# A decoder layer in fp32 on one core: both gates' projections as seven half-size products instead of eight

## The chip, the core and the metric

One core of one Trainium2 chip runs the kernel. The metric is the device time of one execution in microseconds (us), the median over the runs; lower is better. The engines are called as in the profile: PE (matrix products; PEld is its loading of stationary operands), DVE (VectorE), ACT (ScalarE), POOL (GpSimd) and SP (here only a queue that issues transfers). Transfers go through queues of SP, ACT and POOL to 16 DMA engines; POOL's queue can add to the target (an accumulating transfer).

## The reference

One layer, 512 tokens (S), 2048 channels, all in fp32:

```python
h   = RMSNorm_pre(x)
[q | k | v | z_att | u | g_glu | z_conv] = h @ w_in      # 2048 x 7168, seven parts of 1024 columns
# group A: stick-breaking attention, 8 heads x 128
y_att  = attention(q, k, v) * silu(z_att)
# group B: GLU(u, g_glu) -> causal depthwise conv (31 taps) -> LayerNorm -> silu -> pointwise
y_conv = conv_module(u, g_glu) * silu(z_conv)
out = x + RMSNorm_post(concat(y_att, y_conv) @ w_out)
```

The change concerns `h @ z_att` and `h @ z_conv`, the two gates.

## The kernel before, in words

**Products.** PE multiplies in a reduced fp32 form. So each operand is split into a high part and the rest (`split`: ACT writes `h_*`, DVE subtracts and writes `l_*`), and a product is three matmuls (`mm3`): high by high, high by low, low by high. h is kept so in `h_hi` and `h_lo`, channels on partitions, 512 tokens in the free dimension.

**Steps.** The work of PE is a list of steps, each with a load and two units. A step's load brings 1 MB of weights by SP's queue into one of two buffers (`raws`), and splits it into one of two buffers each of `his` and `los`; the load of step n+1 is written ahead of the units of step n. `pair(c0, ...)` makes 256 output channels: channels on the partitions of the result, weights stationary (128x128), h streaming 512 tokens. A pair is two steps (two halves of the 2048 input channels) of 48 matmuls 128x512. Each gate is four pairs (`za0` to `za3` by `gates_a`, `zc0` to `zc3` by `gates_c`), so the gates are 16 steps and 768 matmuls. `post_za` takes a finished result through Silu on ACT and multiplies the attention's `o_raw` on POOL; `post_zc` puts Silu of the result into `szc`, which the pointwise product takes later.

**Strassen's products elsewhere.** The values v and the output product were made by Strassen's seven products already: the matrices are cut into 2x2 blocks, and seven products of sums of blocks take the place of eight. Sums of weights are made in DRAM (`plan_sums`) by POOL's queue, a copy and then an accumulating transfer for each 1 MB; `sum_next` writes the next one of a list where it is called, not ahead of the latest matmul. v's sums of h (`make_v_form`) are made in SBUF (`xw`) by DVE.

**Order.** PE's order is the order of the code. That of DVE, ACT and POOL comes from a scheduler, by priorities: loads have a high one, work in the background list `bgq` a low one (`LATER`). In `bgq` are the 30 taps for each of eight channel tiles of the conv (DVE, `acc`, L401) and the LayerNorm. Four entries are taken per unit before `n_norm`, two behind it. Attention for each head (`heads_run`) goes forward by one tick per unit. The steps follow each other so: u and g, q and k, the 14 steps of v, more of g, u, q, k (`heads(t)`, `conv_in(t)`), the gates from `za0`, `za1`, `zc0`, `za2`, then from `n_norm` `zc1`, `zc2`, `zc3`, `za3` with the LayerNorm beside, four pointwise steps (`pw`), and 28 steps of output products (`a` and others, weights `r_w`, sums `ws`).

Names in rows: `r_x`, `h_x`, `l_x` are a weight block x as loaded and its two parts; `vs`, `ws` are sums of weights for v and for the output; `gn`, `xT`, `gT` belong to the start; `sz` is a gate after Silu.

Of the kernel before, what the change touches and what calls it, by code (L numbers as in the profile page):

```python
# [16 lines left out]
P = 128  # L17
# [27 lines left out]
SUMS_FROM = 18  # L45
# [3 lines left out]
def hybrid_layer(  # L49
# [46 lines left out]
    def split(hi, lo, src, scale=None):  # L96
# [4 lines left out]
        else:  # L101
# [3 lines left out]
            )  # L105

# [281 lines left out]
    def post_u(c):  # L388
        def post(i, ps):
# [29 lines left out]
    def mean_of(src, name):  # L419

        hi, lo = late(f"{name}_hi", F32R), late(f"{name}_lo", F32R)
        split(hi, lo, src)
        ps = op2.tile([P, S], F32, tag="o2", name=f"ln_{name}")
        nc.tensor.matmul(ps, mean_w, hi, start=True, stop=False)
        nc.tensor.matmul(ps, mean_w, lo, start=False, stop=True)
        return ps

    def layer_norm():

        mu = mean_of(ln_sums[0], "mu")  # L430
        yield
# [9 lines left out]
        var = mean_of(sqs[0], "var")  # L441
        v, y, t = late("ln_v"), late("ln_y"), late("ln_t")
# [49 lines left out]
    def plan_sums(name, order, pairs, block):  # L492

        made, todo = {}, deque()
        for q in order:
            base, more = SUMS[q]
            for accumulate in (False, True):
                for p in range(pairs):
                    for kg in range(2):
                        def go(q=q, base=base, more=more, accumulate=accumulate, p=p, kg=kg):  # L500
                            if accumulate:
                                return nc.gpsimd.dma_start(
                                    made[q, p, kg], block(*more, p, kg), accum_op=ALU.add
                                )
# [27 lines left out]
    V_ORDER = (1, 2, 5, 6, 3, 7, 4)  # L532
# [14 lines left out]
    def make_v_form(q):  # L547

        tt = nc.vector.tensor_tensor
        for mi in range(2):  # L550
            for jj in range(2):
# [21 lines left out]
                v_form[q, mi, jj] = hi, lo  # L573
                split(hi, lo, f)
# [30 lines left out]
    def v_load(q, kg):  # L605
        name = f"v{q}{kg}"
        ahead = min(2000, tc.cur_priority - floor[0])
        with tc.high_priority(offset=ahead):
# [4 lines left out]
            split(hi, lo, raw)  # L613
        form = {(1, 0): 5, (2, 1): 6, (6, 1): 3, (3, 0): 7}.get((q, kg))
# [127 lines left out]
    def post_za(h):  # L742
        def post(i, ps):
            sz = t2(f"sz{h + i}")
            nc.scalar.activation(sz, ps, AF.Silu)
            o = o_raw[h + i]
            nc.gpsimd.tensor_tensor(out=o, in0=o, in1=sz, op=ALU.mult)
        return post

    szc = {}  # L750

    def post_zc(c):
        def post(i, ps):
            szc[c + i] = t2(f"szc{c + i}")
            nc.scalar.activation(szc[c + i], ps, AF.Silu)
        return post


    def pointwise(t):
        def unit(i):  # L760
            def go(w):
# [4 lines left out]
                for k in range(CT):  # L766
                    mm3(ps, (hi[:, k, cs], lo[:, k, cs]), (s_hi[k], s_lo[k]), k == 0, k == CT - 1)
                yc = szc[c]
                nc.vector.scalar_tensor_tensor(
                    out=yc, in0=ps, scalar=vec[:, c, V_PB : V_PB + 1], in1=yc,  # L770
# [252 lines left out]
    def gates_a(t):  # L1023
        pair(C_ZA + t * 256, post_za(2 * t), f"za{t}")
# [270 lines left out]
```

## Time and profile before

| what | us |
|---|---|
| median of 3 runs | 870.19 (869.29 to 872.12) |
| the profiled execution | 871.51 |
| its span | 869.8, granted clock 0.997 |
| PE busy | 855.0 (98%), 3894 instructions |
| DVE busy | 631.0 (73%) |
| ACT busy | 395.3 (45%) |
| POOL busy | 124.5 (14%) |
| the gates' stage (481.50 to 664.70) | 183.20 long: PE busy 183.20, DVE 97.80, ACT 84.34, DMA engines 0.49 of it |

The profile is of one execution, so its own time stands beside the span of its instructions. Busy shares are means over stages; what a stage can give is read from its own row. A matmul's record overlaps the next one's, so what it costs in a row of many is the distance of the starts.

### The profile page before, as it was taken

The page shows a single profiled execution, that of the slowest core. Times are in us where ns is not written, and L with a number is a line of the kernel's source. Part 1 is how long each engine was busy: PE and PEld are TensorE (multiplying, and loading weights), DVE is VectorE, ACT ScalarE, POOL GpSimd, SP SyncE. Part 2 cuts the span into 40 slices and gives each one's busy share as a digit, 9 for nine tenths or more (in the row PEclk, how much of TensorE's full clock was granted, in tenths as well). Part 3 has the DMA queues.
Part 4 walks back from the last instruction along what each step waited for, and adds up shares of the span by engine and source line. Part 5 has one row for each costly group of instructions (what it writes and reads, how often), then busy time and mean ns, then how long its engine had stood idle before and what let it go on. Part 6 is the DMA issues. An engine that isn't in the chain of part 4 may idle for free.

```text
span 869.8 us, 9834 instructions
## 1 busy us (share of the span) xinstructions
PE 855.0 (98%) x3894; PEld 710.0 (82%) x3894; DVE 631.0 (73%) x773; ACT 395.3 (45%) x452; POOL 124.5 (14%) x154
## 2 busy tenths in 40 slices
PE   9999998999999999999999999999999999999995
PEld 7888787888888888888888888888888888888884
DVE  4798799986797979879696984245643776458775
ACT  5785124644443544243422545235722346455542
POOL 0221100001202132203111323031001000000031
PEclk9999999999999999999999999999999999999998
DMA  8899964568578455874488547862232346556783
GB/s 324 250 272 283 281 158 160 185 207 302 173 181 174 165 193 145 179 189 165 145 192 165 176 157 183 175 162 97 93 101 97 98 154 233 194 194 250 289 279 101
DMA packets 87046, 163.58 MB, mean 188 GB/s; under 512 B 3014, under 2 KB 52434, under 8 KB 83224
## 3 DMA queue, kind: packets, MB, share of 16 engines
q1 hardware_dynamic: 69824, 110.12, 37.3%
q0 software_dynamic: 16864, 52.43, 26.1%
q8 instruction: 30, 0.49, 0.2%
q10 hardware_dynamic: 312, 0.40, 0.1%
q14 instruction: 16, 0.13, 0.0%
HBM read 158.75 MB, written 54.53 MB: 245 GB/s over the span
## 4 chain that ended last, share of the span: by engine, by line
PE 80%; DVE 10%; DMA 6%; ACT 2%; issue 1%; POOL 0%; DVEq 0%; ACTq 0%; POOLq 0%
PE za L342 3%; PE zc L342 3%; PE za L344 3%; PE a L940 3%; PE zc L344 3%; PE za L343 3%; PE a L942 3%; PE zc L343 3%; PE a L941 3%; DVE acc L401 3%; DVE l_v L100 3%; DMA r_k<-in_w_in_dram 3%; PE k L342 3%; PE q L344 3%; PE q L342 3%; PE u L344 3%
## 5 line engine op out<-in xcount | busy, mean ns | idle before, releaser
L401 DVE SCALAR_TENSOR_TENSOR acc<-hg,vec,acc 128x512 f32<-128x512 f32 x240 | 182.2, 759 | 6.8
L100 DVE TENSOR_TENSOR l_w<-r_w,h_w 128x2048 fp32r<-128x2048 f32 x28 | 64.1, 2291 | 41.9 <-ACT h_w L99 41.9
L99 ACT ACTIVATE h_w<-r_w 128x2048 fp32r<-128x2048 f32 x28 | 53.5, 1915 | 42.1 <-DMA r_w<-ws 11.8
L344 PE MATMUL k<-h_hi,l_k 128*128 128x512 f32 x128 | 50.1, 391 | 1.1 <-DVE l_k L100 1.1
L342 PE MATMUL u<-h_hi,h_u 128*128 128x512 f32 x128 | 50.3, 393 | 0.0
L342 PE MATMUL q<-h_hi,h_q 128*128 128x512 f32 x128 | 50.1, 392 | 0.0
L342 PE MATMUL k<-h_hi,h_k 128*128 128x512 f32 x128 | 50.0, 391 | 0.0
L342 PE MATMUL za<-h_hi,h_za 128*128 128x512 f32 x128 | 50.0, 390 | 0.0
L342 PE MATMUL zc<-h_hi,h_zc 128*128 128x512 f32 x128 | 49.9, 390 | 0.0
L344 PE MATMUL u<-h_hi,l_u 128*128 128x512 f32 x128 | 49.9, 390 | 0.0
L344 PE MATMUL q<-h_hi,l_q 128*128 128x512 f32 x128 | 49.9, 390 | 0.0
L344 PE MATMUL za<-h_hi,l_za 128*128 128x512 f32 x128 | 49.8, 389 | 0.0
L344 PE MATMUL zc<-h_hi,l_zc 128*128 128x512 f32 x128 | 49.8, 389 | 0.0
L343 PE MATMUL u<-h_lo,h_u 128*128 128x512 f32 x128 | 49.8, 389 | 0.0
L343 PE MATMUL k<-h_lo,h_k 128*128 128x512 f32 x128 | 49.8, 389 | 0.0
L343 PE MATMUL za<-h_lo,h_za 128*128 128x512 f32 x128 | 49.8, 389 | 0.0
L343 PE MATMUL q<-h_lo,h_q 128*128 128x512 f32 x128 | 49.8, 389 | 0.0
L343 PE MATMUL zc<-h_lo,h_zc 128*128 128x512 f32 x128 | 49.8, 389 | 0.0
L940 PE MATMUL a<-h_w,f_hi 128*128 128x512 f32 x128 | 49.8, 389 | 0.0
L941 PE MATMUL a<-l_w,f_hi 128*128 128x512 f32 x128 | 49.8, 389 | 0.0
L942 PE MATMUL a<-h_w,f_lo 128*128 128x512 f32 x128 | 49.8, 389 | 0.0
L671 POOL TENSOR_SCALAR_AFFINE_SELECT t<-t 128x128 f32<-128x128 f32 x64 | 35.7, 635 | 81.1 <-DVE t L694 48.2
(339 smaller groups left out, 2136.7 us busy)
## 6 DMA issues: line engine op xcount, KB each, us to landing
ws<-in_w_out_dram POOLq DMA_DIRECT2D x24, 1024.0 KB, 9.3
r_w<-ws SPq DMA_DIRECT2D x16, 1024.0 KB
vs<-in_w_in_dram POOLq DMA_DIRECT2D x12, 1024.0 KB, 12.9
r_w<-in_w_out_dram SPq DMA_DIRECT2D x12, 1024.0 KB
r_u<-in_w_in_dram SPq DMA_DIRECT2D x8, 1024.0 KB
r_q<-in_w_in_dram SPq DMA_DIRECT2D x8, 1024.0 KB
r_k<-in_w_in_dram SPq DMA_DIRECT2D x8, 1024.0 KB
r_v<-vs SPq DMA_DIRECT2D x8, 1024.0 KB
```

The costliest lines, as they stand in the source:

```text
L99: nc.scalar.activation(hi, src, AF.Copy)
L100: nc.vector.tensor_tensor(out=lo, in0=src, in1=f32(hi), op=ALU.subtract)
L342: nc.tensor.matmul(ps, wh, ah, start=first, stop=False)
L343: nc.tensor.matmul(ps, wh, al, start=False, stop=False)
L344: latest[0] = nc.tensor.matmul(ps, wl, ah, start=False, stop=last).ins
L401: bgq.append(lambda j=j: nc.vector.scalar_tensor_tensor(out=acc, in0=hg[:, j : j + S], scalar=vec[:, ct, j : j + 1], in1=acc, op0=ALU.mult ...
L671: nc.gpsimd.affine_select(out=blk, in_=blk, compare_op=ALU.is_gt, fill=0.0, base=0, pattern=[[-1, P]], channel_multiplier=1,)
L940: nc.tensor.matmul(ps, fh[:, kk, ts], hi[:, k, :], start=st, stop=False, skip_group_check=True)
L941: nc.tensor.matmul(ps, fh[:, kk, ts], lo[:, k, :], start=False, stop=False, skip_group_check=True)
L942: nc.tensor.matmul(ps, fl[:, kk, ts], hi[:, k, :], start=False, stop=en, skip_group_check=True)
```

## The change

Both gates are made by Strassen's seven products, in step: products of the first gate ("a") and the second ("c") alternate in an order that lets both use one sum of h (`Z_ORDER`). Each is two steps of 24 matmuls: 28 steps, 672 matmuls 128x512. Now h is stationary (128 tokens) and 512 columns of weights stream, so tokens lie on the partitions of the result. `z_done` combines results (copies on ACT, sums on DVE), and `turn_z` transposes the four finished blocks of a gate on PE, 64 transposes in 16 groups, each followed by Silu and, for gate a, two multiplications on POOL.

The sums of h that the products need (forms 5, 6, 3, 7) are those of v. They are written to DRAM when v makes them (`kept_form`, 16 transfers of 256 KB by ACT's queue), loaded again in the gates by SP (`load_form`, 16 transfers) and split in place over `h_hi` and `h_lo` (`split_form`).

Sums of weights: forms 5 and 7 afresh (`begin`, then `take_up`), form 6 and then 4 "grown" in the place of form 5 or 6 by one accumulating transfer after that was loaded. For v this leaves 12 transfers instead of 16, for the output 28 instead of 32, and the gates add 24. Besides: a weight block is split in two halves (`split_halves`) in v and in the gates; the first tap of each conv tile goes from DVE to ACT; `conv_in(3)` stands after `heads(3)`, so that the last two tiles' taps fall into the gates; the LayerNorm begins at the 16th of the gates' steps, its matmuls some entries after their operands; pointwise takes its channels in the order 2, 3, 0, 1; v begins with form 5.

```diff
+    def split_halves(hi, lo, src):
+        half = src.shape[1] // 2
+        for a in (0, half):
+            split(hi[:, a : a + half], lo[:, a : a + half], src[:, a : a + half])
...
-            bgq.append(lambda: nc.vector.tensor_scalar(
-                out=acc, in0=hg[:, 0:S], scalar1=vec[:, ct, 0:1],
+            bgq.append(lambda: nc.scalar.activation(
+                acc, hg[:, 0:S], AF.Identity, bias=vec[:, ct, V_CB : V_CB + 1],
...
+        grown = {SUMS[q][0]: q for q in (6, 4) if q not in fresh}
+        def loaded_sum(q, p, kg, queue):
+            if q in grown:
+                made[grown[q], p, kg] = made[q, p, kg]
+                queue.append(partial(take_up, grown[q], p, kg))
...
-    V_ORDER = (1, 2, 5, 6, 3, 7, 4)
+    V_ORDER = (5, 1, 2, 6, 3, 7, 4)
...
+                nc.scalar.dma_start(
+                    kept_form[q][:, 4 * jj : 4 * jj + 4, mi * P : (mi + 1) * P], f
+                )
                 split(hi, lo, f)
...
+    Z_ORDER = [(1, "a"), (2, "a"), (5, "a"), (1, "c"), (5, "c"), (2, "c")]
+    Z_ORDER += [(q, which) for q in (6, 3, 7, 4) for which in "ac"]
+    Z_FORMS = {
+        (1, "a", 1): (5, 0, 1), (5, "c", 1): (6, 0, 0), (6, "a", 1): (3, 2, 0), (6, "c", 1): (7, 0, 1),
+    }
...
+    def load_form(q, j0, half):
+        for n in range(4):
+            raw = t2(f"r_form{q}{n}").rearrange("p (k t) -> p k t", k=2)
+            with tc.high_priority(offset=LATER):
+                nc.sync.dma_start(raw, kept_form[q][:, 2 * n : 2 * n + 2, :])
+            splits.append((z_units[0] + 4, partial(split, h_hi[j][:, ks, ts], h_lo[j][:, ks, ts], raw)))
...
+    def z_load(q, which, kg):
+            nc.sync.dma_start(
+                raw, z_w(which)(*PLAIN[q], 0, kg) if q in PLAIN else z_sum[which][q, 0, kg]
+            )
+            split_halves(hi, lo, raw)
+        z_loaded[which](q, 0, kg, zgrow)
+        if (q, which, kg) in Z_FORMS:
+            load_form(*Z_FORMS[q, which, kg])
...
+    def z_done(q, which, i):
+        if q in (1, 5, 4):
+            nc.scalar.copy(nat(q), ps)
+        elif q == 2:
+            tt(out=nat(1), in0=ps, in1=nat(1), op=ALU.add)
+        elif q == 6:
+            tt(out=nat(6), in0=nat(5), in1=ps, op=ALU.subtract)
...
+    def turn_z():
+        for c in range(2):
+            for i in range(2):
+                nc.tensor.transpose(
+                    ps[:, c * 256 + i * P : c * 256 + (i + 1) * P],
+                    z_nat[base, which, i][:, (2 * c2 + c) * P : (2 * c2 + c + 1) * P], ident,
+                )
+        nc.scalar.activation(sz, ps, AF.Silu)
...
+            for k in range(4):
+                ah, al = h_at(4 * (j0 + kg) + k, t0, t0 + P)
+                nc.tensor.matmul(ps, ah, hi[:, k, :], start=st, stop=False, skip_group_check=True)
+                nc.tensor.matmul(ps, ah, lo[:, k, :], start=False, stop=False, skip_group_check=True)
+                latest[0] = nc.tensor.matmul(ps, al, hi[:, k, :], start=False, stop=en, skip_group_check=True).ins
...
     heads(2)
+    heads(3)
     conv_in(3)
-    heads(3)
-    gates_a(0)
...
-    gates_a(3)
+    n_gates = len(steps)
+    gates()
+    n_norm = n_gates + 8
+    n_ln = n_gates + 15
     n_in = len(steps)
-    for t in range(4):
+    for t in (2, 3, 0, 1):
...
-        if n >= SUMS_FROM:
-            sum_next(sumq)
+        if SUMS_FROM <= n < n_gates or n >= n_in:
+            sum_next(zsumq or sumq)
+            if n % 3 == 0 or n >= n_in:
+                sum_next(zsumq or sumq)
...
             sum_next(v_sumq)
+            sum_next(grow)
+            sum_next(zgrow)
```

What this does to the order of the instructions at three places.

DVE in the gates, before: behind the last taps its work is almost only the splits of the weight blocks `l_za..` and `l_zc..` (the two digits are pair and half), one of the attention's (`al7`) and the LayerNorm's.

```order
L100 TENSOR_TENSOR l_zc01_4027<-r_zc01_4025,h_zc01_4026 128x2048
L100 TENSOR_TENSOR l_za20_4099<-r_za20_4097,h_za20_4098 128x2048
L100 TENSOR_TENSOR al7_4093<-aT7_4081,ah7_4092 128x1280
L100 TENSOR_TENSOR l_za21_4173<-r_za21_4171,h_za21_4172 128x2048
L100 TENSOR_TENSOR mu_lo_4330<-ln_sum_1703,mu_hi_4329 128x512
L100 TENSOR_TENSOR l_zc10_4230<-r_zc10_4228,h_zc10_4229 128x2048
L100 TENSOR_TENSOR l_zc11_4300<-r_zc11_4298,h_zc11_4299 128x2048
```

And now, in the first half of the gates (the digits of `l_zc50` are product and half; `acc6`, `acc7` are the conv's taps of the last two tiles, `r_form60` a piece of form 6, which is split over `h_hi0` and `h_lo0`):

```order
L100 TENSOR_TENSOR l_zc50_4113<-r_zc50_4111,h_zc50_4112 128x1024 x2
L406 SCALAR_TENSOR_TENSOR acc6_3679<-hg6_3676,vec_126,acc6_3679 128x512
L406 SCALAR_TENSOR_TENSOR acc7_3711<-hg7_3708,vec_126,acc7_3711 128x512
L406 SCALAR_TENSOR_TENSOR acc6_3679<-hg6_3676,vec_126,acc6_3679 128x512
L406 SCALAR_TENSOR_TENSOR acc7_3711<-hg7_3708,vec_126,acc7_3711 128x512
L406 SCALAR_TENSOR_TENSOR acc6_3679<-hg6_3676,vec_126,acc6_3679 128x512
L406 SCALAR_TENSOR_TENSOR acc7_3711<-hg7_3708,vec_126,acc7_3711 128x512 x3
L100 TENSOR_TENSOR l_zc51_4171<-r_zc51_4169,h_zc51_4170 128x1024 x2
L406 SCALAR_TENSOR_TENSOR acc7_3711<-hg7_3708,vec_126,acc7_3711 128x512 x2
L100 TENSOR_TENSOR h_lo0_120<-r_form60_4177,h_hi0_116 128x2x256
L406 SCALAR_TENSOR_TENSOR acc7_3711<-hg7_3708,vec_126,acc7_3711 128x512
L100 TENSOR_TENSOR h_lo0_120<-r_form61_4179,h_hi0_116 128x2x256
```

The splits stand as two halves for every 24 matmuls of PE, and between them are now taps and pieces of forms, which stood elsewhere or nowhere.

PE between the two units of the step `zc50`, now: the last of the first unit's matmuls, a group of transposes of gate a's first finished block, and the second unit.

```order
L898 MATMUL zc50_4185<-h_zc50_4112,h_hi0_116 128x512
L899 MATMUL zc50_4185<-l_zc50_4113,h_hi0_116 128x512
L900 MATMUL zc50_4185<-h_zc50_4112,h_lo0_120 128x512
L872 MATMUL zTa00_4199<-ident_91,zna10_3801 128x128
L872 MATMUL zTa00_4199<-ident_91,zna11_3868 128x128
L872 MATMUL zTa00_4199<-ident_91,zna10_3801 128x128
L872 MATMUL zTa00_4199<-ident_91,zna11_3868 128x128
L898 MATMUL zc51_4208<-h_zc50_4112,h_hi0_116 128x512
```

Before, a unit was 24 matmuls of a pair and the next unit followed at once; now it is 12, with such a group after 16 of the units.

POOL from the end of the gates on, before: the last multiplications by the gate (`o4`, `o5`, then `o6`, `o7`), the LayerNorm's sums and then only the end of the program (`xr`).

```order
L502 DMA ws710_3847<-in_w_out_dram 512x1x512
L502 DMA ws711_3962<-in_w_out_dram 512x1x512
L747 TENSOR_TENSOR o4_3248<-o4_3248,sz4_4258 128x512
L747 TENSOR_TENSOR o5_3520<-o5_3520,sz5_4285 128x512
L438 TENSOR_TENSOR ln_sq0_4336<-ln_sq0_4336,ln_sq2_4338 128x512
L438 TENSOR_TENSOR ln_sq0_4336<-ln_sq0_4336,ln_sq4_4340 128x512
L438 TENSOR_TENSOR ln_sq0_4336<-ln_sq0_4336,ln_sq6_4342 128x512
L747 TENSOR_TENSOR o6_3922<-o6_3922,sz6_4830 128x512
L747 TENSOR_TENSOR o7_4168<-o7_4168,sz7_4857 128x512
L1011 TENSOR_TENSOR xr0_6081<-r_0_1_5493,xr0_6081 128x512
```

And now, behind the last multiplications, in the pointwise and first output steps:

```order
L885 TENSOR_TENSOR o3_2929<-o3_2929,sza11_5082 128x256
L513 DMA ws610_3475<-in_w_out_dram 512x1x512
L513 DMA ws611_3477<-in_w_out_dram 512x1x512
L518 DMA ws700_5196<-in_w_out_dram 512x1x512
L518 DMA ws701_5198<-in_w_out_dram 512x1x512
L518 DMA ws710_5260<-in_w_out_dram 512x1x512
L518 DMA ws711_5262<-in_w_out_dram 512x1x512
L513 DMA ws700_5196<-in_w_out_dram 512x1x512
L513 DMA ws701_5198<-in_w_out_dram 512x1x512
L513 DMA ws710_5260<-in_w_out_dram 512x1x512
L513 DMA ws711_5262<-in_w_out_dram 512x1x512
L513 DMA ws600_3338<-in_w_out_dram 512x1x512
```

Ten transfers of 1 MB (copies at L518, accumulations at L513) that stood before the gates' end stand there now, and four more accumulations follow them.

More of the change, by code (lines that the diff above doesn't have):

```diff
@@ L422, in mean_of, with finish @@
         split(hi, lo, src)
[L423 to L426, printed above, removed]
+        def finish():
+            ps = op2.tile([P, S], F32, tag="o2", name=f"ln_{name}")
+            nc.tensor.matmul(ps, mean_w, hi, start=True, stop=False)
+            nc.tensor.matmul(ps, mean_w, lo, start=False, stop=True)
+            return ps
+        return finish
     def layer_norm():
         mu = mean_of(ln_sums[0], "mu")
+        for _ in range(4):
+            yield
+        mu = mu()
         yield
@@ L441, in layer_norm @@
         var = mean_of(sqs[0], "var")
+        for _ in range(5):
+            yield
+        var = var()
         v, y, t = late("ln_v"), late("ln_y"), late("ln_t")
@@ new lines, in hybrid_layer @@
+    for which in "ac":
+        z_sum[which], todo, z_loaded[which] = plan_sums(f"z{which}", (5, 7), 1, z_w(which))
+        zsumq.extend(todo)
+    def load_form(q, j0, half):
+        ts = slice(half * (S // 2), (half + 1) * (S // 2))
+        for n in range(4):
+            raw = t2(f"r_form{q}{n}").rearrange("p (k t) -> p k t", k=2)
+            with tc.high_priority(offset=LATER):
+                nc.sync.dma_start(raw, kept_form[q][:, 2 * n : 2 * n + 2, :])
+            j, ks = j0 + n // 2, slice(n % 2 * 2, n % 2 * 2 + 2)
+            splits.append((
+                z_units[0] + 4, partial(split, h_hi[j][:, ks, ts], h_lo[j][:, ks, ts], raw)
+            ))
@@ new lines, in turn_z @@
+    def turn_z():
+        if not turns or turns[0][0] > z_units[0]:
+            return
+        _, which, base, c2, pr, half = turns.popleft()
+        ps = op2.tile([P, S], F32, tag="o2", name=f"zT{which}{pr}{half}")
+        for c in range(2):
[3 more added lines that the diff above has]
+                    z_nat[base, which, i][:, (2 * c2 + c) * P : (2 * c2 + c + 1) * P], ident,
+                )
+        sz = t2(f"sz{which}{pr}{half}")
+        nc.scalar.activation(sz, ps, AF.Silu)
+        sz = sz.rearrange("p (c t) -> p c t", c=2)
+        if which == "c":
+            szc[pr, half] = sz
+            return
+        ts = slice(half * 256, (half + 1) * 256)
+        for c in range(2):
+            o = o_raw[2 * pr + c][:, ts]
+            nc.gpsimd.tensor_tensor(out=o, in0=o, in1=sz[:, c, :], op=ALU.mult)
@@ L759, in pointwise, with gates @@
+    def gates():
+        for q, which in Z_ORDER:
+            for kg in range(2):
+                steps.append(Step(
+                    lambda q=q, which=which, kg=kg: z_load(q, which, kg),
+                    [z_unit(q, which, kg, 0), z_unit(q, which, kg, 1)],
+                ))
     def pointwise(t):
@@ L767, in go @@
                     mm3(ps, (hi[:, k, cs], lo[:, k, cs]), (s_hi[k], s_lo[k]), k == 0, k == CT - 1)
-                yc = szc[c]
-                nc.vector.scalar_tensor_tensor(
-                    out=yc, in0=ps, scalar=vec[:, c, V_PB : V_PB + 1], in1=yc,
-                    op0=ALU.add, op1=ALU.mult,
-                )
+                for half in range(2):
+                    yc = szc[c // 2, half][:, c % 2, :]
+                    nc.vector.scalar_tensor_tensor(
+                        out=yc, in0=ps[:, half * 256 : (half + 1) * 256],
+                        scalar=vec[:, c, V_PB : V_PB + 1], in1=yc, op0=ALU.add, op1=ALU.mult,
+                    )
             return go
@@ L785, in y_raw @@
     def y_raw(k, half):
-        t = o_raw[k] if k < CT else szc[k - CT]
-        return t[:, half * HT : (half + 1) * HT]
+        if k < CT:
+            return o_raw[k][:, half * HT : (half + 1) * HT]
+        return szc[(k - CT) // 2, half][:, k % 2, :]
     def make_form(q):
@@ L1235, in hybrid_layer @@
         if n == n_norm:
+            assert not heads_ready and len(o_raw) == NH
             att.close()
-            conv_stack.close()
             op2 = ctx.enter_context(
@@ L1240, in hybrid_layer @@
             )
+        if n == n_ln:
+            assert not bgq
+            conv_stack.close()
             late_stack = ExitStack()
```

143 lines of the change are left out of this document (95 added, 48 removed).

## The prediction

> **What bounds the kernel now.** I read the busy times first, then the shares of the chain that ended last, then busy time by stage, then the rows of the costliest groups.
>
> ```profile
> PE 855.0 (98%) x3894; PEld 710.0 (82%) x3894; DVE 631.0 (73%) x773; ACT 395.3 (45%) x452; POOL 124.5 (14%) x154
> PE 80%; DVE 10%; DMA 6%; ACT 2%; issue 1%; POOL 0%; DVEq 0%; ACTq 0%; POOLq 0%
> 0.00:62.45 62.45, 60.65 (x298) 50.69 (x299) 44.74 (x104) 44.30 (x89) 10.04 (x21) 1.00 0.93 285
> 62.45:129.00 66.55, 65.41 (x293) 53.28 (x292) 57.34 (x83) 21.22 (x24) 7.44 (x10) 1.00 0.94 245
> 129.00:208.00 79.00, 76.21 (x334) 62.05 (x333) 70.68 (x76) 41.26 (x42) 2.94 (x4) 1.00 0.58 196
> 208.00:481.50 273.50, 273.50 (x1283) 229.56 (x1283) 225.28 (x247) 106.93 (x87) 54.66 (x79) 1.00 0.68 178
> 481.50:664.70 183.20, 183.20 (x830) 152.41 (x829) 97.80 (x97) 84.34 (x91) 35.06 (x35) 1.00 0.49 138
> 664.70:708.50 43.80, 43.80 (x195) 36.27 (x194) 27.61 (x41) 14.14 (x16) 2.91 (x1) 1.00 0.29 96
> 708.50:861.00 152.50, 152.20 (x672) 125.70 (x670) 103.45 (x121) 82.30 (x106) 11.28 (x6) 1.00 0.63 223
> 861.00:869.80 8.80, 0.00 (x0) 0.00 (x0) 4.07 (x10) 0.83 (x4) 0.19 (x1) 0.67 0.63 200
> ```
>
> The columns of a stage are its length, then the busy time of PE, PEld, DVE, ACT and POOL, the granted clock, the share of time in which the DMA engines worked, and GB/s. The stages are the start, u and the first q and k, the values, the middle, the gates (481.50 to 664.70), the pointwise products, the output products and the tail. PE stands idle for 1.1 us in the second and 2.8 us in the third, 3.9 together, and never in the gates. There a matmul left out is time off the end, as long as VectorE (97.8 of 183.2 us) and the transfers (0.49) stay within what is left. The change spends both reserves, so they are what must be costed.
>
> **TensorE.** How far one gate matmul is from the next, the last of the gates against the next after it:
>
> ```profile
> 664.48 0.39 PE L344 MATMUL za<-h_hi,l_za 128*128 128x512 f32 x1
> 664.70 0.39 PE L342 MATMUL pw<-s_hi,h_pw 128*128 128x512 f32 x1
> 664.93 0.39 PE L343 MATMUL pw<-s_lo,h_pw 128*128 128x512 f32 x1
> 60.53 2.17 PE L1212 MATMUL gT<-ident,g_nat 128*128 128x128 f32 x16
> 62.45 0.48 PE L342 MATMUL u<-h_hi,h_u 128*128 128x512 f32 x1
> 12.80 0.60 PE L237 MATMUL xT<-ident,x 128*128 128x128 f32 x4
> 13.15 0.48 PE L471 MATMUL gn<-h_gn,h_hi 128*128 128x512 f32 x1
> 13.47 0.40 PE L472 MATMUL gn<-l_gn,h_hi 128*128 128x512 f32 x1
> ```
>
> Starts are 0.22 and 0.23 us apart; I take 0.227. Seven products instead of eight make 672 matmuls of 128x512 out of 768: 96 x 0.227 = 21.8 us fewer. Weights and h change places, but both forms load 128x128 and stream 512, so the pitch is the same. Added are 64 transposes of 128x128 in 16 groups of four. Sixteen in a row took 1.92 us from 60.53 to 62.45, 0.12 each; a group of four amid matmuls took 0.35 to the next matmul, whose own start to the one after was 0.32 instead of 0.23, so 0.44 a group: 7.0 us (by 0.12 each, 7.7). Net -14.8 us. No other product changes its count.
>
> **VectorE in the gates.**
>
> ```profile
> L401 DVE SCALAR_TENSOR_TENSOR acc<-hg,vec,acc 128x512 f32<-128x512 f32 x240 | 182.2, 759 | 6.8
> L100 DVE TENSOR_TENSOR l_za<-r_za,h_za 128x2048 fp32r<-128x2048 f32 x8 | 18.4, 2300 | 31.7 <-ACT h_za L99 31.7
> L100 DVE TENSOR_TENSOR s_lo<-acc,s_hi 128x512 fp32r<-128x512 f32 x8 | 5.1, 683 | 0.0
> L401 DVE SCALAR_TENSOR_TENSOR acc<-hg,vec,acc 128x512 f32<-128x512 f32 x24 | 19.9, 831 | 0.6
> L694 DVE SCALAR_TENSOR_TENSOR t<-z,t 128x1280 f32<-128x1280 f32 x2 | 3.0, 1487 | 3.8 <-ACT t L693 3.8
> L702 DVE TENSOR_TENSOR_SCAN t<-t 128x512 f32<-128x512 f32 x2 | 3.4, 1720 | 0.0
> 47.11 0.60 DVE h_lo L245
> 47.71 0.60 DVE l_gn L100
> L99 ACT ACTIVATE h_za<-r_za 128x2048 fp32r<-128x2048 f32 x8 | 15.3, 1917 | 41.9 <-PE zc L343 17.5 <-PE k L343 14.5 <-PE za L343 9.8
> L745 ACT ACTIVATE sz<-za 128x512 f32<-128x512 f32 x8 | 4.7, 590 | 8.2 <-PE za L344 8.2
> L502 POOL DMA_DIRECT2D ws<-in_w_out_dram x4 | 4.7, 1174 | 27.2 <-PE o_ps L344 12.7 <-PE za L344 12.0 <-PE zc L344 2.5
> ```
>
> The rows with x24, x2 and x4 are of the gates' stage alone, the others of the whole run; the two short ones are pieces of the chain. Of its 97.8 us, 15 splits of 128x2048 go (34.5) and one head's softmax, which now comes before (7, half of what its six groups have there, of which the first and the longest scan are shown). Added: 28 weight blocks in two halves each. No row has 128x1024; between 0.68 (512) and 2.30 (2048) by elements it is 1.22, so 56 make 68.3. Sixteen splits of h's combinations and sixteen combinations of products, 512 wide, at 0.68 make 21.8. The order has 60 taps there instead of 24, since conv_in(3) now stands after the last heads: 36 x 0.76 = 27.4. The sum is 174 us for about 200 instructions. But their records overlap: 512-wide ones are recorded with 0.68 and start 0.60 apart in the two pieces of the chain, so 200 x 0.08 = 16 goes off: 158 us, in a stage of 183.2 - 14.8 = 168. That is 0.94. The nearest row is the values' stage, 70.7 of 79 (0.89) with 24-matmul steps as here, where PE lost 2.8; scaled to 168 us that is 6. Since much of that loss lay at its first loads and since halves let a step's first matmuls start on half a block, I take 2.5, between 0 and 6 (a gain is excluded: PE has no idle time there to give back).
>
> ScalarE gets the other part of every split (15 x 1.92 become 56 of, between its rows by elements, 1.03), 12 copies, 16 form splits and two first taps at 0.59: its 84.3 us become 131 of 168, so it is not the bound. POOL has eight multiplications as sixteen of half the width, equal work, and about as many transfers to issue (8, at up to 1.17). The 16 Silu come again as 16. Between them and the end only the last `a4` and `c4` groups stand, and pointwise now begins with channels whose `szc` are longest done, so their latency (transpose, Silu) is covered by 40 us of pointwise products; without that cover it would be about 2 us once.
>
> **Transfers.** Bytes, and what became of loads where the queue of accumulated sums was full:
>
> ```profile
> q1 hardware_dynamic: 69824, 110.12, 37.3%
> q0 software_dynamic: 16864, 52.43, 26.1%
> 60.00:70.00 10.00, 9.96 (x58) 8.03 (x57) 10.00 (x24) 9.80 (x16) 2.71 (x3) 1.00 1.07 220
> 90.00:100.00 10.00, 10.00 (x46) 8.29 (x45) 9.68 (x12) 0.00 (x0) 0.00 (x0) 1.00 1.09 337
> 100.00:110.00 10.00, 8.89 (x40) 7.05 (x39) 5.46 (x6) 3.52 (x3) 2.34 (x2) 1.00 1.00 228
> 58.12 19.88 DMA r_q<-in_w_in_dram
> 82.38 21.91 DMA r_k<-in_w_in_dram
> 143.73 6.36 SPq L612 DMA_DIRECT2D r_v<-vs  x2
> 106.34 2.29 DVE L100 TENSOR_TENSOR l_k<-r_k,h_k 128x2048 fp32r<-128x2048 f32 x1 [4.44 <-ACT h_k L99]
> ```
>
> 37.3% of 869.8 us over 110.12 MB is 2.95 us of all engines a megabyte for loads; 26.1% over 52.43 is 4.3 for POOL's sums (an average of copies and accumulations). In the gates stand 28 loads, 4 MB of kept forms (together 94 us) and 8 accumulations (35 at 4.3, up to 52 if one costs 6.5, since it reads its target too, three megabytes moved where a copy moves two): 130 to 147 of 168, a share of 0.77 to 0.87 against 0.49 now. A load took about 6 us alone (the last row but one, two issues; l_v follows) and some 20 each, in flight together, where the share was 1.07 to 1.09; there l_k came 4.44 us late and PE lost 1.1. With two buffers, one is reused after load, one half on ScalarE (1.03) and two on VectorE (2 x 1.14, with the overlap off): 6 + 1.03 + 2.28 = 9.3 per two steps, which last 2 x 24 x 0.227 = 10.9. The spare is 1.6 us. I add 1.0 us for the two places where forms and accumulations meet (from 0 to 12, below). With VectorE's 2.5 the gates' term is +3.5.
>
> [...]
>
> At pointwise and the first output products ten sums of POOL's are issued which before were done by then. At 4.3 each they are 43 us of the engines in a stretch where the share is 0.29; between 0 and 5 (a 20-us load once, as above, against 10.9-us steps, costs 1 to 5): +2. The sums of the middle stage are about 30 where 24 were; they meet a share of 0.68 and steps of 10.9 us, so I cost them at 0; if that cover goes, they come late into the same ten.
>
> **The early stages.** Before the values only 8 transfers make `vs` now, not 16, so r_k and r_v come sooner; against that ScalarE issues 16 writes of h's combinations (4 MB, 12 us of the engines), which VectorE's next write to the same buffer must await, with conv taps queued behind. Between -3.9 (all idle time found) and +3 (a wait as l_k's in each of three forms, PE paying a quarter): I take -2.5, since half the traffic at the one late load is removed.
>
> **Sum:** 871.51 - 14.8 + 3.5 + 2 - 2.5 = 859.7 for the profiled execution, which lay 1.3 over the median of 870.19; so 858.4, say 858.
>
> **The rivals.** *All is covered:* gates, pointwise and early stages lose nothing: 870.2 - 14.8 - 3.9 = 851.5. For it: PE lost nothing in 273 us of the middle with VectorE at 0.82. Against it: 0.94.
>
> *VectorE is the bound in the gates:* the durations count in full where an instruction must wait for the one before it, as in the chain of taps (0.76 to 0.83 in the rows above, not 0.68). Then 174 us against 168 gives +6, and as work is not even over the steps, some 3 more: 870.2 - 14.8 + 9 + 2 - 2.5 = 864.
>
> *The transfers are the bound, and it is slower:* a load needs 2.95 us of the engines in 5.45 us, a share of 0.54. If sums and forms in flight leave it less, each step waits. It decides from there: at a third, a load takes 8.9 us and loses 3.4 a step; one burst (2 MB of forms and four accumulations, 32 us of the engines at two thirds, so 48 us or 5.4 loads) costs 18 us. One burst so and the other at half price: 27, and the pointwise ones at 5, make 870.2 - 14.8 - 2.5 + 27 + 5 = 885; the first alone makes 873. For it: the 20-us loads. Against it: in 50 us at a share above 1.0 PE lost 1.1 only, if with 10.9-us steps.
>
> **How the numbers follow.** What a measurement of this kernel can tell from no change is 0.3%, 2.6 us, so "same" is 867.6 to 872.8. My forecast (854 to 863) gets 0.52, all covered 0.14 (851 to 854), VectorE the bound 0.19 (862 to 869), transfers the bound 0.15 (866 to 885). Faster is 0.52 + 0.14 + 0.16 + 0.01 = 0.83, same 0.03 + 0.04 = 0.07, slower 0.10. The range 851 to 869 leaves out most of the last case and the lower edge of the second, under 2 in 10.
>
> **What the next profile would show.** PE busy about 840 with 3862 instructions or so. The gates' stage 168 to 174 us, its DVE busy near 165. If PE's idle time there follows `l_z` halves that follow `h_z`, with r_z landing over 8 us after issue, it is the transfers; if `l_z` follows DVE's own taps, it is VectorE. r_k and r_q landing under 15 us bear out the early term; idle time at L344 pw or the first a products with 1.2-us POOL issues beside it bears out the +2. I am wrong if the softmax of heads 6 and 7, which must end eight steps into the gates, holds PE's hand-written order, or if the accumulating transfers move at another price than the mean.

## The result and the profile after

The changed kernel takes 916.46 us (median of 4 runs, 915.17 to 917.9) against 870.59 us before: 1.0536 times as long, 95% interval 1.0501 to 1.0571. The forecast was 858. The profiled execution took 915.17 us, its span is 913.5.

First the busy times, the chain's shares and the two large queues, as shown of before:

```profile
PE 856.6 (94%) x3862; PEld 704.4 (77%) x3862; DVE 672.7 (74%) x859; ACT 432.8 (47%) x536; POOL 149.4 (16%) x178
...
PE 38%; DVE 18%; DMA 17%; issue 4%; ACT 4%; POOL 1%; SPq 0%; DVEq 0%; ACTq 0%; POOLq 0%
...
q1 hardware_dynamic: 64128, 126.90, 40.2%
q0 software_dynamic: 27232, 69.21, 34.7%
```

PE executes 32 instructions less, as the prediction counted, and yet is busy longer (856.6 us, 855.0 before). The chain was PE for 80% and is for 38%; transfers went from 6% to 17%. POOL's sums went from 52 to 69 MB, and cost 317 us of the engines (34.7% of 913.5) instead of 227.

Then the stages, cut at the first matmul of each: start, u with q and k, values, middle, gates, pointwise, output, tail. Cut so, the stages of before begin at 62.45, 130.5, 210.3, 481.5, 664.7 and 708.2 us and its tail at 860.7; the rows in the prediction are cut up to 2.3 us earlier at the values and the middle.

```profile
0.00:62.00 62.00, 60.19 (x299) 49.97 (x299) 44.45 (x104) 43.76 (x88) 10.47 (x20) 1.00 0.93 287
62.00:129.10 67.10, 66.50 (x299) 54.52 (x298) 61.30 (x88) 23.70 (x27) 1.28 (x2) 1.00 0.67 187
129.10:213.40 84.30, 79.25 (x337) 64.51 (x336) 68.49 (x82) 42.85 (x55) 5.63 (x6) 0.96 0.81 232
213.40:487.00 273.60, 272.46 (x1283) 228.68 (x1283) 201.99 (x213) 114.72 (x96) 65.09 (x93) 1.00 0.74 198
487.00:686.50 199.50, 175.07 (x781) 141.56 (x780) 161.87 (x195) 110.67 (x145) 40.82 (x37) 0.96 0.70 208
686.50:731.00 44.50, 44.50 (x201) 36.83 (x200) 21.82 (x34) 11.76 (x11) 7.67 (x8) 1.00 0.99 271
731.00:904.50 173.50, 158.64 (x673) 128.31 (x671) 108.75 (x135) 84.21 (x110) 17.93 (x12) 0.95 0.79 241
```

| stage | before | after | change | forecast |
|---|---|---|---|---|
| start, u, q, k, values | 210.3 | 213.4 | +3.1 | -2.5 |
| middle | 271.2 | 273.6 | +2.4 | 0 |
| gates | 183.2 | 199.5 | +16.3 | -11.3 |
| pointwise and output | 196.0 | 218.0 | +22.0 | +2 |
| tail | 9.1 | 9.0 | -0.1 | 0 |
| span | 869.8 | 913.5 | +43.7 | -11.8 |

PE is idle for 24.4 us of the gates and 14.9 of the output, where it lost nothing before. DVE is busy for 161.9 of 199.5 in the gates, near the count, but not full. What PE waited for, from the view of waits (total us, times, longest):

```profile
PE za L898 <- ACT h_za L99: 12.3, 2, 10.6
PE a L1102 <- ACT h_w L99: 8.6, 1, 8.6
PE vb L666 <- ACT h_v L99: 4.6, 1, 4.6
PE za L899 <- DVE l_za L100: 4.4, 3, 2.9
PE zc L898 <- ACT zna L849: 4.0, 1, 4.0
```

And four pieces of the chain (start, length):

```profile
162.32 13.85 DMA r_v<-in_w_in_dram
524.19 11.51 DMA r_zc<-in_w_in_dram
592.61 18.17 DMA r_form<-kept
735.32 18.49 DMA r_w<-in_w_out_dram
```

Behind each of the four longest waits on ACT stands a load of 11 to 18 us. What ACT waited for was not always the block that PE needed. Its rows at the longest wait, of 10.6 us:

```profile
606.47 0.63 ACT L99 ACTIVATE h_hi<-r_form 128x512 fp32r<-128x512 f32 x1 [10.87 <-DMA r_form<-kept]
...
611.34 1.99 ACT L99 ACTIVATE h_za<-r_za 128x1024 fp32r<-128x1024 f32 x2
```

The split of `r_za`, which PE needs, stands behind three pieces of a form (the rows of the second and third would stand at the dots) and starts without a wait of its own, 4.87 us behind the first of them. In the same way the copy `zna` stood behind the split of `r_zc`.

What the DMA engines did meanwhile, by queue (packets, MB, share of 16 engines) between 592.6 and 611 us; q0 carries the last accumulations of a burst of four (issued at 576.7 to 594.1 us), q1 the loads of SP:

```profile
q0 software_dynamic: 1277, 2.52, 74.2%
q1 hardware_dynamic: 1127, 2.16, 35.3%
```

The loads get 35% of the engines (packets of the two queues overlap in the records, so the shares come to 1.10). At that share 1 MB takes 2.95 / 0.353 = 8.4 us, and a step of the gates is 5.45 us long.

### The profile page after: what moved, and what is told of

It is laid out like the page before. It is cut to its first block, busy times and chain, and to the rows that moved or that the text cites. A ratio compares the mean times of both kernels' runs of the same rounds, so it can differ in the third digit from the quotient of the medians.

```text
span 913.5 us, 10104 instructions
## 1 busy us (share of the span) xinstructions
PE 856.6 (94%) x3862; PEld 704.4 (77%) x3862; DVE 672.7 (74%) x859; ACT 432.8 (47%) x536; POOL 149.4 (16%) x178
## 3 DMA queue, kind: packets, MB, share of 16 engines
q0 software_dynamic: 27232, 69.21, 34.7%
## 4 chain that ended last, share of the span: by engine, by line
PE 38%; DVE 18%; DMA 17%; issue 4%; ACT 4%; POOL 1%; SPq 0%; DVEq 0%; ACTq 0%; POOLq 0%
DVE acc L406 5%; DMA r_form<-kept 4%; DMA r_w<-in_w_out_dram 4%; DVE l_w L100 3%; DMA r_w<-ws 3%; ACT h_w L99 2%; DMA r_g<-in_w_in_dram 2%; DVE l_za L100 2%; PE k L347 2%; PE q L348 2%; PE k L349 2%; PE pw L348 2%; PE q L349 2%; PE pw L347 2%; PE k L348 2%
## 5 line engine op out<-in xcount | busy, mean ns | idle before, releaser
L1102 PE MATMUL a<-h_w,f_hi 128*128 128x512 f32 x128 | 51.8, 405 | 8.6 <-ACT h_w L99 8.6
L898 PE MATMUL za<-h_za,h_hi 128*128 128x512 f32 x112 | 45.5, 406 | 12.3 <-ACT h_za L99 12.3
L703 POOL TENSOR_SCALAR_AFFINE_SELECT t<-t 128x128 f32<-128x128 f32 x64 | 41.1, 736 | 88.2 <-DVE t L726 59.6
L1103 PE MATMUL a<-l_w,f_hi 128*128 128x512 f32 x128 | 51.7, 404 | 3.4 <-DVE l_w L100 3.4
L898 PE MATMUL zc<-h_zc,h_hi 128*128 128x512 f32 x112 | 46.2, 412 | 6.6 <-ACT zna L849 4.0
L899 PE MATMUL za<-l_za,h_hi 128*128 128x512 f32 x112 | 44.6, 399 | 4.4 <-DVE l_za L100 4.4
L99 ACT ACTIVATE h_v<-r_v 128x1024 fp32r<-128x1024 f32 x28 | 28.1, 1051 | 40.9 <-DMA r_v<-in_w_in_dram 13.2
L899 PE MATMUL zc<-l_zc,h_hi 128*128 128x512 f32 x112 | 44.9, 401 | 1.1 <-DVE l_zc L100 1.1
L900 PE MATMUL zc<-h_zc,h_lo 128*128 128x512 f32 x112 | 44.9, 401 | 0.0
## 6 DMA issues: line engine op xcount, KB each, us to landing
vs<-in_w_in_dram POOLq DMA_DIRECT2D x12, 1024.0 KB, 11.7
```

What stands on the lines that cost most here:

```text
L99: nc.scalar.activation(hi, src, AF.Copy)
L898: nc.tensor.matmul(ps, ah, hi[:, k, :], start=st, stop=False, skip_group_check=True)
L899: nc.tensor.matmul(ps, ah, lo[:, k, :], start=False, stop=False, skip_group_check=True)
L900: latest[0] = nc.tensor.matmul(ps, al, hi[:, k, :], start=False, stop=en, skip_group_check=True).ins
L1102: nc.tensor.matmul(ps, fh[:, kk, ts], hi[:, k, :], start=st, stop=False, skip_group_check=True)
L1103: nc.tensor.matmul(ps, fh[:, kk, ts], lo[:, k, :], start=False, stop=False, skip_group_check=True)
```

## The experiments

Theory A: accumulations take two thirds of the DMA engines, and weight loads with a third don't keep up with steps of 24 matmuls. Theory B: VectorE, nearly full in the gates, is what PE waits for.

**Take each suspect away.** Four kernels leave transfers out of the changed one, so that what they compute lacks those sums or forms.

```diff
  e1
-            sum_next(zgrow)
  e2
-            sum_next(grow)
+        if n == n_in:
+            left = [f for f in sumq if f.func.__name__ == "begin"]
+            sumq.clear()
+            sumq.extend(left)
  e3
...
-                nc.sync.dma_start(raw, kept_form[q][:, 2 * n : 2 * n + 2, :])
...
+            raw = f32(h_hi[j][:, ks, ts])
  e4: e1, e2, e3, and the accumulations for v
```

> Leaves out the 8 accumulating transfers of the gates, so products 6 and 4 of both gates take the sums of products 5 and 6 instead. Theory A (the accumulations take two thirds of the DMA engines and the weight loads beside them get one third): the waits of PE on h_za, h_zc and r_form at 534, 562, 568 and 602 us (4.0, 0.7, 1.9, 10.6 us) go, with most of the 6.7 us that the lower clock costs after them: the gates' stage 199.5 -> about 178 us, the whole 916 -> about 896. Theory B (VectorE, 0.94 full by the count, is what PE waits for): only 2 to 4 us go, the whole 912 to 915.

Measured 894.35 us. The row of its gates:

```profile
488.60:668.20 179.60, 169.78 (x782) 138.22 (x781) 162.55 (x195) 110.85 (x145) 34.62 (x29) 1.00 0.53 185
```

Eight accumulations less, and the stage is 19.9 us shorter; PE's idle time falls from 24.4 to 9.8. In the runs below that leave the gates' transfers as they are (e2, f2, f3) the stage took 199.2 to 202.1 us, so the difference is far beyond what runs differ by.

> Leaves out the accumulations that stand behind the gates for the output's weights (the ones of forms 6 and 7 not made by then, and the four grown ones); the copies of form 7 stay. Theory A: the waits of PE on h_w and l_w (8.6, 1.5, 0.6, 1.8 and 1.8 us, and the clock behind them) go, and the output stage comes back from 173.5 to about 153 us: the whole 916 -> about 896. Theory B says nothing of this stage; were the output stage slow because its operands come late from the last gate blocks, it would stay at about 170 us.

Measured 895.62 us. Its output stage has its old length, with no idle time of PE:

```profile
733.80:886.20 152.40, 152.40 (x673) 125.89 (x671) 108.67 (x135) 84.90 (x110) 10.95 (x6) 1.00 0.63 223
```

All 21.0 us by which this stage had grown went with the late accumulations.

> Leaves out the 16 loads of h's kept combinations in the gates; the 16 splits stay, from what stands in h_hi. Theory A: 4 MB of 2.95 us less in front of weight loads, half of it in bursts that get a third of the engines: the gates lose 8 to 12 us of their 24 us of idle time, the whole 916 -> 903 to 908. Theory B: no change, 914 to 917.

Measured 900.12 us, gates 184.7: the forms' loads cost 14.8 us where accumulations are in flight, more than expected. They and the eight accumulations share one loss, so the two differences don't add up. PE's idle time in the gates says the same: 9.8 us with the forms' loads alone, 11.0 with the accumulations alone, 24.4 with both and, in the next run, 3.1 with neither.

> Leaves out all of these and the eight accumulations for v, so that nearly only plain loads and copies are left. Theory A: what is left is PE's count and VectorE: gates 168 to 174 us, values 79 to 80, output 153, the whole 858 to 866, that is, the forecast's sum without its transfer terms. Theory B: the gates stay at 185 us or more, the whole 875 or more.

Measured 859.21 us, 0.9863 times the time before (0.9828 to 0.9897). Its stages: u with q and k, values, gates.

```profile
62.00:129.10 67.10, 66.52 (x299) 54.58 (x298) 61.52 (x88) 23.76 (x27) 0.13 (x1) 1.00 0.44 142
129.10:205.50 76.40, 76.40 (x338) 63.02 (x337) 68.30 (x83) 43.10 (x55) 2.12 (x3) 1.00 0.61 206
478.70:651.90 173.20, 170.11 (x781) 139.67 (x780) 158.10 (x190) 108.18 (x141) 32.96 (x29) 0.99 0.49 168
```

VectorE does the same here but for the source of the form splits (158.1 of 173.2, 0.91), and PE waits for 3.1 us in the gates. Theory B is out as the cause of the loss; at most these 3.1 us are left to it.

**The dose, in the kernel before.** Sixteen accumulations that nothing uses, eight beside steps of 48 matmuls, eight beside steps of 24:

```diff
+        for first in (n_norm, n_pw + 6):
+            if first <= n < first + 8:
+                q, kg = (5, 6, 7, 4)[(n - first) // 2], (n - first) % 2
+                sum_next(deque([lambda: nc.gpsimd.dma_start(
+                    v_sum[q, 0, kg], v_w(0, 0, 0, kg), accum_op=ALU.add)]))
```

> The kernel before, with 16 accumulations more that nothing uses (onto the values' sums after those were loaded): 8 in the gates, one for each of eight steps of 48 matmuls (10.9 us), and 8 in the output stage, one for each of eight steps of 24 (5.45 us). Theory A, by bytes: load and accumulation want 2.95 + 6.0 = 8.95 us of the DMA engines a step; beside 10.9 us this costs nothing (gates 183 to 184), beside 5.45 us it costs up to 8 x 3.5 = 28 less what two buffers and the stage's free time give back: output stage 152.5 -> 165 to 180, the whole 871 -> 884 to 899. If accumulations cost as such (a fixed price each), both stages grow alike.

Measured 886.29 us (1.0178, 1.0159 to 1.0196). Its gates and its output:

```profile
479.60:662.70 183.10, 183.10 (x830) 152.35 (x829) 97.91 (x97) 84.23 (x89) 44.37 (x43) 1.00 0.76 183
706.30:876.00 169.70, 156.62 (x673) 126.49 (x671) 103.37 (x121) 81.57 (x105) 20.49 (x14) 0.98 0.82 249
```

Eight accumulations cost nothing beside 10.9-us steps and 17.2 us beside 5.45-us steps. That the changed kernel made h stationary, or transposed anything, isn't needed for the loss.

The two eights were not spread alike, though. In the gates POOL issued one a step, 575 to 652 us; in the output it issued all eight at once, not one a step as was meant:

```profile
706.73 9.47 POOL L1256 DMA_DIRECT2D vs<-in_w_in_dram  x8 [38.63 <-PE pw L344]
```

So this run alone doesn't tell the length of the steps from the burst. Two others do. In the changed gates without the forms' loads (e3) eight were issued over 73 us, 10.4 us apart on average, nearly as here in the gates, and that stage took 184.7 us where it took 173.2 without them (e4): 11.5 us beside 5.45-us steps. And in the run f2 below POOL's queue held 68% of the engines for 273 us beside 10.9-us steps, and PE lost nothing by it.

**Packets or bytes?** The gates' accumulations take a second operand that lies in one piece, h's kept form 6, and leave the weight block out:

```diff
-                queue.append(partial(take_up, grown[q], p, kg))
+                queue.append(partial(take_up, grown[q], p, kg) if other is None else lambda: nc.gpsimd.dma_start(
+                    made[q, p, kg].rearrange("p k c -> p (k c)"), other.rearrange("p k c -> p (k c)"), accum_op=ALU.add, max_dma_last_dim=8192))
...
-        z_sum[which], todo, z_loaded[which] = plan_sums(f"z{which}", (5, 7), 1, z_w(which))
+        z_sum[which], todo, z_loaded[which] = plan_sums(f"z{which}", (5, 7), 1, z_w(which), kept_form[6])
```

> The 8 accumulations of the gates take their second operand from 1 MB that lies in one piece (h's kept form 6 in place of the weight block), so that they go in rows of 8 KB instead of 2 KB. Theory P (an accumulation is dear because its packets are small: 176 ns for 2 KB against 84 ns for a load's): its price falls from 6.0 to about 4 us of all engines per MB, and the gates' stage from 199.5 to 185 to 192 us. Theory R (it is dear because it reads its target too, and the price goes by bytes): 6 us stay, gates 198 to 201, the whole 914 to 918.

Measured 910.51 us; the gates took 200.3. The queues between 590.6 and 609 us, and then only up to 602, while accumulations were in flight nearly throughout:

```profile
q0 software_dynamic: 289, 2.10, 55.0%
q1 hardware_dynamic: 1631, 3.35, 47.5%
...
q0 software_dynamic: 258, 1.97, 83.5%
q1 hardware_dynamic: 310, 0.82, 19.3%
```

An accumulation costs 0.550 x 18.4 / 2.10 = 4.8 us of the engines per MB in rows of 8 KB and 0.742 x 18.4 / 2.52 = 5.4 in rows of 2 KB (above): 11% less, and nothing for the stage. The price went mostly by bytes. While they were in flight the loads had 19% of the engines here, against 35% with rows of 2 KB; they caught up when the accumulations were over. The span is 5.0 us shorter: 3.7 of it lie in the values' stage (80.6 us, where other runs of its code had 84.3 to 85.4) and 1.7 in the output, which the edit does not touch; why is open.

**Put the sums elsewhere.** All sums for the output made afresh and but three issued ahead of the gates:

```diff
-    w_sum, sumq, w_loaded = plan_sums("ws", (5, 6, 7), 2, w_block)
+    w_sum, sumq, w_loaded = plan_sums("ws", (5, 6, 4, 7), 2, w_block)
...
-            if n % 3 == 0 or n >= n_in:
+            if len(sumq) > 4 or n >= n_in:
```

> Nothing is left out; the sums for the output's weights are all made afresh (none grown, 32 transfers) and but three of them issued before the gates, two per step instead of four in three steps. If accumulations cost only where steps are 24 matmuls long (5.45 us) and nothing where they are 48 (10.9 us): output stage 152.5 to 154, the middle 273 to 276, the whole 916 -> 895 to 899. If the middle is then full (24 copies at 2.9, 21 accumulations at 6.0 and 26 loads at 2.95 make 273 us of its 273): output 153, but the middle 10 to 20 us longer, the whole 905 to 916.

Measured 892.92 us, 2 us under what was expected. Its middle with POOL's queue there, and its output:

```profile
213.50:487.00 273.50, 272.35 (x1284) 228.64 (x1282) 202.42 (x213) 114.73 (x96) 75.18 (x107) 1.00 0.96 258
q0 software_dynamic: 15410, 46.07, 68.0%
731.40:883.80 152.40, 152.40 (x673) 125.89 (x671) 108.62 (x135) 84.55 (x110) 10.94 (x6) 1.00 0.63 223
```

The middle, with 48 matmuls a step, takes all of it at a share of 0.96 and is no longer than in the changed kernel. The gates keep their loss (199.8 us).

**One gate only.** z_conv by seven products with all sums made ahead, z_att by pairs; conv_in(3) where it was, and at first the values' order and sums of before:

```diff
-    Z_ORDER = [(1, "a"), (2, "a"), (5, "a"), (1, "c"), (5, "c"), (2, "c")]
+    Z_ORDER = [(q, "c") for q in (1, 2, 5, 6, 3, 7, 4)]
...
-    n_gates = len(steps)
+    for t in range(4):
+        pair(C_ZA + t * 256, post_za(2 * t), f"za{t}")
+    n_gates = n_norm = n_ln = len(steps)
     gates()
-    n_norm = n_gates + 8
...
```

> Nothing is left out: only z_conv by seven products, all its sums made afresh ahead of it, z_att by pairs as before (48 matmuls a step, so the sums go on beside it); values, their sums and the place of conv_in(3) as before; no accumulation beside steps of 24 matmuls but three at pointwise. TensorE: 48 matmuls less (-10.9) and 8 groups of transposes more (+3.5), so 870.6 - 7.4 = 863; with 0 to 4 us of waits for h's forms and VectorE, 863 to 867. If loads of forms alone suffice to stall steps of 24 matmuls (as in the run without the gates' accumulations, 9.8 us of idle time in two gates): 868 to 872.

Measured 874.3 us, above both ranges expected. Its gates took 177.1 us, 6.1 less than before and less than both gates without their accumulations (179.6); but the stage ahead of the values took 77.5 instead of 67.1. The same order of the values in the changed kernel:

> The values' order and sums as before (all four sums afresh, made ahead, v begins with plain blocks), the rest changed. The values' stage 84.3 -> 79 to 80 as before, the one ahead of it 67.1 -> 68: the whole 916 -> 912 to 914. If the 4 MB of kept forms cost there too, it stays above 80.

Measured 917.56 us, not 912 to 914: values 76.4, but 79.8 ahead of them, with a wait of 9.4 us on `h_q`. The loss had moved by one stage. Three placings of the values' sums in the one-gate kernel followed:

> Nothing is left out: one gate by seven products as in the run with one gate, but the values as in the changed kernel (form 5 first, sums 6 and 4 grown). If the 7.7 us wait on h_q at 96 us of the run with one gate came from the sums for v and the kept writes in flight together: the stage ahead of the values 77.5 -> 67 to 68, the values' stage 76.4 -> 84 (the grown sums beside 24-matmul steps), the whole 874 -> 871 to 873. If the kept writes alone did it, the stage ahead stays above 72.

> Nothing is left out: as the run before, but the sum of form 4 of the values is made ahead by a copy of form 5 and two accumulations, in the stretch 80 to 125 us where the changed kernel's DMA engines are at 0.3 to 0.9; only form 6 is grown, early in the values. If what stalls is accumulations beside 24-matmul steps: stage ahead 67 to 70, values 76 to 78, gates 177, output 152.5, the whole 861 to 866, faster than both. If the early stretch then fills as in the run with one gate: 868 to 874.

> Nothing is left out: as the run with one gate and mixed sums, but the copy and the two accumulations for form 4 of the values begin only in the second step of q (about 95 us), when the kept writes of form 5 are over. If those two in flight together made the 9.3 us wait on h_q: the stage ahead of the values 67 to 69, values 76.4 to 80, gates 177, the whole 861 to 866. If the sums meet the kept writes of form 6 instead, the values' stage stays at 82 or more: 868 to 872.

Measured 870.38, 879.48 and 872.9 us; stage ahead and values 67.1 and 85.4, 80.9 and 78.6, 67.1 and 85.7. So sums made early stall the one and sums made late the other. The second and the third were expected at 861 to 866, and lay even above what was given for the case that a stall stayed (868 to 874 and 868 to 872). What stalls the earlier stage was still open. ACT's and its queue's rows at 94 to 107 us of the second of the three:

```profile
95.40 9.37 ACTq L616 DMA_DIRECT2D kept<-xw  x3
104.89 1.91 ACT L99 ACTIVATE h_q<-r_q 128x2048 fp32r<-128x2048 f32 x1 [15.27 <-DVE acc L406]
...
DVE xw L599 <- DMA kept<-xw: 11.7, 2, 6.3
```

Three writes of h's forms are issued over 9.4 us, and `h_q` stands behind them on ACT. The last line, from the view of waits, is why they take so long: twice DVE waits, 11.7 us together, for an earlier write to end before it may fill that buffer (`xw`) again, and ACT cannot issue a write before the sum is there.

> As the run with mixed sums (one gate; form 4 of the values' sums made early), but h's forms are neither written to DRAM nor loaded again (the gate's products take what stands in h). If the writes hold DVE and ACT's queue (11.0 us of idle time ahead of the values): stage ahead 80.9 -> 67 to 69, values 76 to 79. If the accumulations alone delay r_q: it stays at 76 to 81.

Measured 866.86 us. Without the writes (and without the forms), the sums as in the second:

```profile
62.10:129.20 67.10, 66.52 (x299) 54.58 (x298) 60.80 (x89) 23.00 (x27) 5.91 (x6) 1.00 0.88 218
```

80.9 became 67.1: it takes the writes. (The values took 77.8.) The accumulations alone, at a share of 0.88, stall nothing there.

```diff
+            if n >= 2:
+                sum_next(v_four)
+                sum_next(v_four)
```

(`v_four`: a copy of form 5's sum and two accumulations for each half of form 4's.)

> Nothing is left out: one gate; the copies and accumulations for form 4 of the values begin after the first unit of q (about 90 us), two per unit, so that they lie between the writes of form 5 and the 24-matmul steps of v. Theory (only overlap with those two costs): stage ahead 67 to 70, values 76.4 to 79, gates 177, the whole 861 to 866. If there is no free place and they still meet one of the two: 869 to 874.

Measured 867.43 us (12 runs, 866.02 to 867.99), 0.9966 times the time before, 0.9953 to 0.998: the fastest of the complete kernels, if by a third of a per cent, and 1.4 us above the range expected. Its first stage, values and gates:

```profile
62.00:129.10 67.10, 66.51 (x299) 54.55 (x298) 61.23 (x89) 23.79 (x27) 6.94 (x8) 1.00 1.01 263
129.10:208.40 79.30, 77.33 (x337) 62.76 (x336) 68.39 (x83) 42.54 (x55) 3.33 (x4) 1.00 0.76 235
480.70:659.10 178.40, 175.73 (x806) 145.56 (x805) 126.28 (x141) 103.60 (x128) 38.75 (x39) 1.00 0.72 213
```

## Why the prediction was wrong

**TensorE, -14.8: right but for 2.4.** The count fell by 32, and in the kernel without the accumulations and forms PE was busy for 842.6 us instead of 855.0, 12.4 less. The whole came to 859.2, by stages -4.8 up to the values, +2.0 in the middle (ten matmuls of the attention moved there), -10.0 in the gates and +1.0 at pointwise. That this sum, -11.8, is the forecast's is luck: the forecast has 3.0 us for transfers in it that this kernel leaves out, and without them says -14.8. The early part was better, and gates and middle were worse than the terms said.

**VectorE, +2.5: right in kind.** Without the transfers it stood at 158.1 us where the count gave 158, and PE's idle time in the gates was 3.1 us.

**Transfers in the gates, +1.0: this is the step that failed.** The 1.0 was my estimate, and no run shows it; the gates without them took 173.2 us, with them 199.5: 26.3. I had summed what the transfers need over the stage (0.77 to 0.87) and called what is below 1 hidden. But a load wasn't served at the mean share; it got 0.35 while accumulations were in flight, and by the prediction's own sum two buffers left 1.6 us to spare per two steps. Nor had the sum that a split of weights would stand on ACT behind pieces of a form that had not landed, as at the longest wait. The number that decides, a share of 0.54, stood in the third rival with the right third beside it, at a chance of 0.15. I had weighed against it that PE lost only 1.1 us in 50 us of full queues; those were steps of 10.9 us, and the runs that put accumulations beside the one and the other kind of step show that this half of the sentence was the whole matter.

**Pointwise and output, +2: the same step.** I priced the ten sums where they are issued. There PE lost nothing (44.5 us of 44.5), as they have 48 matmuls a step. They landed in the output's steps of 24, and the four grown ones behind them fell there too: +21.0.

**Early stages, -2.5: wrong by sign, +3.1.** r_q and r_k did come in time (u, q, k: 67.1 instead of 68.0). The values lost 5.1 us of idle time to the grown sums of form 4, which I had not placed: `r_v` took 13.85 us beside one, and in the runs that made these sums ahead of the stage it took 76.3 to 79.3 instead of 84.3. The price I gave to the kept writes fell due only where more sums were made early.

**The clock: not in the sum at all.** Of the 26.3 us in the gates 21.3 are idle time, the rest, 5.0, is that matmuls behind a wait ran slower (granted clock 0.96 in the stage); in the output 14.9 of 21.0, and 6.1 (0.95). The foreseen 840 us of PE's busy time came out as 856.6, and as 842.6 where the waits were gone.

**The share that the loads got.** From 592.6 to 611 us the two queues moved 1277 and 1127 packets, not far from equal numbers. A packet of the accumulation took 0.742 x 18.4 x 16 / 1277 = 0.171 us and one of a load 0.353 x 18.4 x 16 / 1127 = 0.092: with equal numbers the loads' part would be 0.092 / 0.263 = 0.35, and they had 0.353 of 1.095, that is 0.32. With rows of 8 KB, from 590.6 to 602 us, it was 258 packets and 310, of 0.590 and 0.114 us; with equal numbers that would be 0.114 / 0.704 = 0.16, and the loads had 0.193 of 1.028, that is 0.19. So in these two stretches the loads' part came near what equal numbers of packets would give; why it did was not shown.

## What to carry to other kernels

Seven half-size products take away an eighth of the matmuls, but each loaded megabyte then serves 24 of them instead of 48: ask what a load may take (the step's length) and what it takes beside the slowest other transfer, not what the mean share is. By what was measured here, an accumulating transfer belongs beside steps that last longer than load and accumulation together (2.95 + 5.4 = 8.4 us): beside steps of 10.9 us it was free, in the middle of f2 at a share of 0.96, and beside steps of 5.45 us eight of them cost 11.5 us (e3 against e4) and 17.2 (m1); no length between was tried. A late transfer can hold up other work too (here ACT waited 10.87 us for a piece of a form, and the split of `r_za`, without a wait of its own, came behind it). A write that an engine must await before it reuses a buffer can hold up what is queued behind it, on the issuing engine too (here three were issued over 9.4 us ahead of `h_q`).

## What the runs showed of the hardware that was not expected

PE's granted clock was lower for some us behind some waits (0.50 from 758 to 763 us) and not behind others (1.00 from 512 to 519). Rows of PE in the changed kernel, around a wait of 2.92 us in the gates and around one of 8.63 in the output:

```profile
512.14 0.50 PE L899 MATMUL za<-l_za,h_hi 128*128 128x512 f32 x1 [2.92 <-DVE l_za L100]
512.48 0.40 PE L900 MATMUL za<-h_za,h_lo 128*128 128x512 f32 x1
512.72 0.40 PE L898 MATMUL za<-h_za,h_hi 128*128 128x512 f32 x1
...
756.14 0.79 PE L1102 MATMUL a<-h_w,f_hi 128*128 128x512 f32 x1 [8.63 <-ACT h_w L99]
...
760.33 0.63 PE L1104 MATMUL a<-h_w,f_lo 128*128 128x512 f32 x1
760.76 0.63 PE L1102 MATMUL a<-h_w,f_hi 128*128 128x512 f32 x1
...
763.32 0.39 PE L1102 MATMUL a<-h_w,f_hi 128*128 128x512 f32 x1
763.55 0.39 PE L1103 MATMUL a<-l_w,f_hi 128*128 128x512 f32 x1
```

The same five microseconds as a stage (its clock is the third figure from the end):

```profile
758.00:763.00 5.00, 4.54 (x11) 3.57 (x12) 4.75 (x6) 2.14 (x3) 0.00 (x0) 0.50 0.66 223
```

Behind the wait of 2.92 us the starts that follow are soon 0.24 us apart; behind that of 8.63 they are 0.43 apart for 5 us at a granted clock of 0.50, then 0.23 again. A wait of 3.97 us was followed by about 3 us at 0.43 (granted clock 0.51 from 538 to 541).

The run without the late accumulations (e2) has nearly the wait of 2.92 us again, at the same place:

```profile
512.34 0.80 PE L899 MATMUL za<-l_za,h_hi 128*128 128x512 f32 x1 [2.90 <-DVE l_za L100]
512.93 0.63 PE L900 MATMUL za<-h_za,h_lo 128*128 128x512 f32 x1
513.36 0.63 PE L898 MATMUL za<-h_za,h_hi 128*128 128x512 f32 x1
```

There starts were 0.43 us apart until 518.5: behind a wait of 2.90 us PE was slower, and behind one of 2.92 it was not. What decides is open.

While loads ran beside it, an accumulating transfer cost the engines 1.8 times a load of the same size (5.4 against 2.95 us per MB).
